# Hybrid encoder layer on one core: both x chunks turned by VectorE blocks and transfers, attention's rows in freed input blocks, queued work weighed by its age

## The chip, the cores and the metric

One NeuronCore of a Trainium2 chip runs the whole layer: a matrix engine (TensorE, PE in the profile), VectorE (DVE), ScalarE (ACT), GpSimd (POOL), and SyncE (SP), whose main job here is to issue transfers. The metric is device microseconds of one execution; the kernel before has a median of 1148.32 us over three runs (1145.85 to 1148.58). One profiled execution of it is read below.

## The reference, cut to what matters

Sequence 256, model width 2048, everything in float32. One layer:

```python
hn = rms_norm(h, g_mix_pre)
q, k, v, xr, yg = split(hn @ w_in, 5 parts of 1024)
attn = neighborhood_attention(q, k, v, rpb)          # 8 heads of 128
rec  = rglru_bidirectional(xr, ...) * gelu(yg)       # conv, gates, forward and backward scan
mixed = concat([rms_norm(attn), rms_norm(rec)]) @ w_out
h = h + rms_norm(mixed)
ff = (silu(fn @ w_ffn_gate) * (fn @ w_ffn_up)) @ w_ffn_down    # fn = rms_norm(h), d_ff 5632
h = h + rms_norm(ff)
h = h + rms_norm(sigmoid(rms_norm(h) @ w_ple_gate) * (p @ w_ple_proj))
```

## The kernel before, in words

**Products.** A float32 product is made of three products of rounded values: the left side and each weight tile are split into a high part (rounded) and a low part (the rest), and hi*hi, lo*hi and hi*lo are added in PSUM. A weight tile is 256 rows by 512 columns (512 KB). It is loaded by SP into one of four raw buffers `wr`; ACT rounds it into `wh` (line 661), DVE subtracts to make `wl` (line 677), and PE uses both in 12 products of 128x512 (lines 715 to 717). There are four pairs of `wh` and `wl`. So a load waits until DVE has split the tile four places ahead of it, and ACT's rounding waits until PE is done with the tile four places ahead. Weight tiles are counted from 0 here, in the order of their use. "Lead" is the time by which a tile's `wl` is ready before PE's first product with it.

**The mixing stage.** The input projection has ten chunks of 512 columns in the order x0 v0 q0 k0 x1 q1 k1 v1 g0 g1; x0 and v0 take turns in tiles 0 to 15, and each later chunk takes eight tiles, up to tile 79. The left side of all of them is `hT_hi`, `hT_lo` (16 blocks of 128 rows). After its last product a chunk is scaled out of PSUM by ACT into `ev` (line 1055, one buffer), and most chunks have to be turned (rows to columns) before they can be used. There are two ways:

- PE turns 128x128 pieces against the identity (line 334, tile `tr`), four pieces for two blocks, into PSUM. x0, x1, k1, g0 and g1 go this way.
- `moved` (lines 340 to 355): DVE turns 32x32 blocks in place (line 343), and 16 small transfers of 32 KB put the blocks in their places in `sq` (line 353, one buffer), all issued by SP. q0, k0 and q1 go this way (`BY_BLOCKS`, line 1028).

A turned x chunk is copied to `xp`, convolved on DVE (`xc`, lines 1106 and 1111), split (`xch`, `xcl`), and its gates are PE products (tile `pg`); their weights are loaded by SP (`av`, line 1083) and split into `gh`, `gl`. Sigmoids, decay, two scans and the sum `hs` follow on ACT and DVE. q and k give scores (`sc`), softmax (`pr`), turned weights of attention (`tr<-ident,pr`), and `po`. When both halves are there, attention's rows are normalised (`attn_norm`) and split: blocks 0 and 1 into `at0`, blocks 2 to 7 into a new pair `attn_hi`, `attn_lo`, which takes the place of `hT_hi`, `hT_lo` as a whole. So its writing waits until the last input product has read them. These rows and the recurrent ones (`rec_hi`, `rec_lo`) are the left side of the output projection, from tile 80 on.

**What sets the order.** Everything is written out once, ahead of time, by a planner (`Plan`, line 91). Streams of work are Python generators that offer their next step with a cost; the planner keeps a clock for PE, DVE, ACT and the transfers, and whenever PE's clock has passed on, it writes every step whose start lies before it, the one with the least start plus `late` first (`_best`, line 152). What it writes is a fixed order for each engine. Small PE work such as `tr`, `pg`, `sc` and `po` is written between weight products once its inputs are planned to be ready. A product costs `MM` = 0.216 us on that clock until the FFN, from where it is 0.2265. A transfer is booked at 150/340 = 0.44 us, and as landed 2.0 us after the last one.

**Pools.** SBUF is nearly full in the mixing stage: its pool `p1` holds `ev` and `sq` once each.

## Time and profile before

| what | value |
|---|---|
| median of three runs | 1148.32 us (1145.85 to 1148.58) |
| span of the profiled execution | 1144.3 us |
| PE busy | 1134.3 us, 99% |
| DVE busy | 945.8 us, 83% |
| ACT busy | 732.1 us, 64% |
| transfers | 269.01 MB, mean 235 GB/s |
| input projection, in the span | to about 255 us |
| output projection | to about 340 us |
| embedding products and the turn to the FFN | 340 to 360 us |
| FFN | to about 1045 us |

The span runs from the first to the last instruction; the median of the runs is 4.0 us above it. PE's instructions overlap in the records (one product starts about every 0.227 us but is shown for 0.39 us), so that PE's busy share hides small pauses; they are found in the waits and in the distances from start to start.

### The profile page before, as it was taken

To read this page: it belongs to the slowest core of one execution; us is meant where nothing else is said; L and a number is where in the kernel's file an instruction comes from. 1 tells how busy PE (TensorE), PEld (TensorE's weight loads), DVE (VectorE), ACT (ScalarE), POOL (GpSimd) and SP (SyncE) were. 2 spreads that over 40 slices of the span, in tenths; PEclk is the share of its full clock that TensorE was granted. 3 is DMA by queue.
4 is the path that set the end of the run, shared out by engine and by line. 5 is a ranking of instruction groups with operands and counts; after the bars stand their busy time and mean duration, and the time that the engine had idled before them with its cause. 6 is when DMAs were issued, how large, how long until landed. Compare 5 with 4: busy or idle time off the path is not lost.

```text
span 1144.3 us, 15197 instructions
## 1 busy us (share of the span) xinstructions
PE 1134.3 (99%) x5175; PEld 942.3 (82%) x5175; DVE 945.8 (83%) x1201; ACT 732.1 (64%) x967; POOL 149.3 (13%) x236
## 2 busy tenths in 40 slices
PE   9999999999999999999999999999999999999997
PEld 7888888888888888888888888888888888888886
DVE  6578697888468779899997898999988888888885
ACT  6777877876447655666566556556564565576674
POOL 0000000000000032132010133232111313100200
PEclk9999999999999999999999999999999999999999
DMA  9867666546685996887877777797797777967862
GB/s 321 288 194 218 180 193 198 167 158 204 208 313 172 300 299 214 230 249 213 279 271 219 260 223 215 249 266 243 258 314 244 229 244 227 285 242 254 257 208 95
DMA packets 110846, 269.01 MB, mean 235 GB/s; under 512 B 36336, under 2 KB 43248, under 8 KB 109360
## 3 DMA queue, kind: packets, MB, share of 16 engines
q1 hardware_dynamic: 96304, 243.17, 63.3%
q0 software_dynamic: 14032, 24.52, 11.2%
q8 instruction: 40, 0.66, 0.2%
q10 hardware_dynamic: 432, 0.35, 0.1%
q14 instruction: 38, 0.31, 0.1%
HBM read 250.17 MB, written 9.44 MB: 227 GB/s over the span
## 4 chain that ended last, share of the span: by engine, by line
PE 92%; DVE 3%; DMA 2%; ACT 2%; issue 1%; SPq 0%; DVEq 0%; ACTq 0%
PE acc L717 23%; PE acc L716 23%; PE acc L715 23%; PE acc L728 7%; PE acc L726 7%; PE acc L727 7%; DVE wl L677 1%; PE tr L334 1%; DMA mg<-part 1%; ACT wh L661 1%; DMA sq<-ev 0%; PE half L2012 0%; PE acc L2012 0%; PE pg L366 0%; PE pg L365 0%
## 5 line engine op out<-in xcount | busy, mean ns | idle before, releaser
L677 DVE TENSOR_TENSOR wl<-wr,wh 128x1024 fp32r<-128x1024 f32 (+1 forms) x300 | 358.9, 1210 | 91.6 <-ACT wh L661 90.2
L661 ACT CAST wh<-wr 128x1024 fp32r<-128x1024 f32 (+1 forms) x300 | 310.8, 1043 | 164.3 <-PE acc L716 112.1
L353 POOL DMA_DIRECT2D mT<-mid x164 | 96.1, 597 | 610.6 <-DMA lower<-in_w_ffn_up 401.1
L716 PE MATMUL acc<-wh,hT_mix_lo 128*128 128x512 f32 x420 | 163.6, 390 | 0.3 <-DVE hT_mix_lo L323 0.3
L715 PE MATMUL acc<-wh,hT_mix_hi 128*128 128x512 f32 x420 | 163.7, 390 | 0.0
L717 PE MATMUL acc<-wl,hT_mix_hi 128*128 128x512 f32 x420 | 163.4, 389 | 0.0
L717 PE MATMUL acc<-wl,hT_hi 128*128 128x512 f32 x320 | 124.5, 390 | 0.0
L715 PE MATMUL acc<-wh,hT_hi 128*128 128x512 f32 x316 | 124.4, 394 | 0.0
L716 PE MATMUL acc<-wh,hT_lo 128*128 128x512 f32 x316 | 123.1, 390 | 0.0
L661 ACT CAST wh<-ple 128x1024 fp32r<-128x1024 f32 (+1 forms) x68 | 68.2, 1008 | 77.4 <-DVE ple L607 47.7
L716 PEld LDWEIGHTS acc<-wh,hT_mix_lo 128*128 128x128 f32 x420 | 78.8, 188 | 17.1 <-DVE hT_mix_lo L323 1.0
L715 PEld LDWEIGHTS acc<-wh,hT_mix_hi 128*128 128x128 f32 x420 | 78.9, 188 | 16.3
L717 PEld LDWEIGHTS acc<-wl,hT_mix_hi 128*128 128x128 f32 x420 | 78.8, 188 | 16.4
L677 DVE TENSOR_TENSOR wl<-ple,wh 128x1024 fp32r<-128x1024 f32 (+1 forms) x68 | 79.2, 1165 | 10.1 <-ACT wh L661 9.7
L717 PEld LDWEIGHTS acc<-wl,hT_hi 128*128 128x128 f32 x320 | 60.0, 188 | 12.8
L716 PEld LDWEIGHTS acc<-wh,hT_lo 128*128 128x128 f32 x316 | 59.4, 188 | 11.6
L715 PEld LDWEIGHTS acc<-wh,hT_hi 128*128 128x128 f32 x316 | 59.4, 188 | 11.4
L630 POOL DMA_DIRECT2D ple<-in_w_ffn_up x27 | 24.1, 892 | 162.9 <-DVE wl L677 121.9
L661 ACT CAST wh<-third 128x1024 fp32r<-128x1024 f32 x33 | 34.7, 1052 | 13.9 <-PE acc L716 8.2
L677 DVE TENSOR_TENSOR wl<-third,wh 128x1024 fp32r<-128x1024 f32 x33 | 40.2, 1219 | 0.7 <-ACT wh L661 0.5
L661 ACT CAST wh<-lower 128x1024 fp32r<-128x1024 f32 x30 | 31.4, 1051 | 13.9 <-PE acc L716 12.4
L677 DVE TENSOR_TENSOR wl<-lower,wh 128x1024 fp32r<-128x1024 f32 x30 | 36.3, 1217 | 1.8 <-ACT wh L661 1.8
(463 smaller groups left out, 2481.1 us busy)
## 6 DMA issues: line engine op xcount, KB each, us to landing
wr<-in_w_in SPq DMA_DIRECT2D x77, 512.0 KB, 4.3
wr<-in_w_ffn_gate SPq DMA_DIRECT2D x73, 512.0 KB, 5.2
wr<-in_w_ffn_down SPq DMA_DIRECT2D x55, 512.0 KB, 5.6
wr<-in_w_ffn_up SPq DMA_DIRECT2D x51, 512.0 KB, 4.8
wr<-in_w_out SPq DMA_DIRECT2D x32, 512.0 KB, 4.4
wr<-in_w_ple_gate SPq DMA_DIRECT2D x30, 512.0 KB, 4.7
lower<-in_w_ffn_up SPq DMA_DIRECT2D x21, 512.0 KB, 5.9
lower<-in_w_ffn_down SPq DMA_DIRECT2D x17, 512.0 KB, 5.7
```

The source lines that it names most:

```text
L334: nc.tensor.transpose(tr[:, b, t * P : (t + 1) * P], e[:, t, sl], ident)
L353: (nc.gpsimd if i in pool else nc.sync).dma_start(dst[32 * j : 32 * j + 32, :, :, i, :], src[32 * i : 32 * i + 32, :, :, j, :],)
L630: nc.gpsimd.dma_start(dst, src, accum_op=ALU.add)
L661: nc.scalar.copy(his[i][:, 0 : src.shape[1], :] if n == 2 else his[i][:, j, :], src)
L677: nc.vector.tensor_tensor(out=los[i][:, m, :], in0=src, in1=f32(his[i][:, m, :]), op=ALU.subtract)
L715: nc.tensor.matmul(accs[t], hi[:, sl], his[i][:, j, :], start=st, stop=False, **group)
L716: nc.tensor.matmul(accs[t], lo[:, sl], his[i][:, j, :], start=False, stop=False, **group)
L717: nc.tensor.matmul(accs[t], hi[:, sl], los[i][:, j, :], start=False, stop=sp, **group)
L726: nc.tensor.matmul(dst, x[0], wh, start=start, stop=False, skip_group_check=seeded)
L727: nc.tensor.matmul(dst, x[1], wh, start=False, stop=False, skip_group_check=seeded)
L728: nc.tensor.matmul(dst, x[0], wl, start=False, stop=stop, skip_group_check=seeded)
```

## The change: what it does

- x0 and x1 are added to `BY_BLOCKS`, so they too are turned by DVE blocks and transfers.
- `ev` and `sq` get a second buffer each (in the pool and in the planner's slots). The room for it comes from the space in SBUF that is reserved for GpSimd's transfer descriptors, which is set to 8192 bytes a partition.
- For all five chunks that are turned by blocks, half of the 16 transfers (`pool=(0, 2)`) are issued by GpSimd instead of SP.
- Attention's rows 2 to 7 are written into blocks 2 to 7 of `hT_hi`, `hT_lo` themselves. Each pair of blocks has an event `ev_used`, set when the last chunk's product with this pair has been written; no new pair is taken.
- The planner lowers `late` of a step by 0.2 times the time that it has been waiting (`age`), until the ninth segment of the output projection. `MM` and `MM4` become 0.2263 and 0.9.

```diff
@@ Plan.__init__
-        self.now = 0.0
+        self.now, self.age = 0.0, 0.2
@@ Plan._best
             late = task.late() if callable(task.late) else task.late
+            late -= self.age * max(0.0, s - task.ready)
             if best is None or s + late < best[0] - 0.05:
@@ layer
-    plan = Plan(wr=R_BUFS, w=W_BUFS, sm=SM_BUFS, acc=4, ev=1, mid=2, bt=2, m2=1, mt=1, sq=1, ...
+    plan = Plan(wr=R_BUFS, w=W_BUFS, sm=SM_BUFS, acc=4, ev=2, mid=2, bt=2, m2=1, mt=1, sq=2, ...
...
-    MM = 0.216
-    MM4 = 0.86
+    MM = 0.2263
+    MM4 = 0.9
@@ products
             if j:
+                if lhs is hT and i >= i_last:
+                    ev_used[kx].t = plan.clk["pe"]
                 free_w(i)
@@ sq_tile
-        return t1["pool"].tile([P, NT, HB, P], F32, tag="sq", name="sq")
+        return t1["pool"].tile([P, NT, HB, P], F32, tag="sq", name="sq", bufs=2)
 
-    BY_BLOCKS = {("q", 0), ("k", 0), ("q", 1)}
+    BY_BLOCKS = {("x", 0), ("x", 1), ("q", 0), ("k", 0), ("q", 1)}
@@ turned
-        eT = yield from moved(e, here, "sq", sq_tile)
+        eT = yield from moved(e, here, "sq", sq_tile, pool=(0, 2))
@@ evac
-                e = t1["pool"].tile([P, NT, N], F32, tag="ev", name="ev")
+                e = t1["pool"].tile([P, NT, N], F32, tag="ev", name="ev", bufs=2)
...
-    ev_in = Event()
+    ev_used = {b: Event() for b in range(0, KD, 2)}
@@ attend
         yield from attn_norm((0,), ra, *at0)
-        yield ev_in
-        at_hi, at_lo = hT_pair("attn")
-        mixT.blocks(at_hi, at_lo, 2, H - 2, 2)
+        mixT.blocks(hT_hi, hT_lo, 2, H - 2, 2)
         for bs in ((2, 6), (4,)):
-            plan.add(attn_norm(bs, ra, at_hi, at_lo), plan.now)
+            plan.add(attn_norm(bs, ra, hT_hi, hT_lo), plan.now)
@@ attn_norm
+            if b:
+                yield ev_used[b]
             yield from split(at_hi[:, sl, :], at_lo[:, sl, :], attnT[:, sl, :], 2 * S)
...
     n_in = len(segs)
+    i_last = len(tiles) - len(KS)
@@ main loop
-            if n == n_in - 1:
-                ev_in.t = plan.clk["pe"]
+            if n == n_in + 8:
+                plan.age = 0.0
@@ kernel
-    nc = bacc.Bacc("TRN2", target_bir_lowering=False, num_devices=1)
+    nc = bacc.Bacc("TRN2", target_bir_lowering=False, num_devices=1, dynamic_dma_scratch_size=8192)
```

The change moves instructions well beyond the lines of the diff, since the planner sets the order. (The diff adds lines, so that line 353 of before is line 354 after, 677 is 678, and so on.)

SP's queue around the turning of x0, before: `wr` are the weight loads, `av` the recurrent gates' weights, `bt` the bias of attention, `sq<-ev` the small transfers, here those of q0.

```order
L578 DMA wr<-in_w_in 128x1024 x11
L1083 DMA av<-in_w_rg_a 128x2x128
L1083 DMA av<-in_w_rg_i 128x2x128
L1083 DMA av<-in_w_rg_a 128x2x128
L1083 DMA av<-in_w_rg_i 128x2x128
L578 DMA wr<-in_w_in 128x1024 x6
L1296 DMA bt<-in_bias 128x2x256 x2
```

The same place after the change, from the same weight load on:

```order
L579 DMA wr<-in_w_in 128x1024 x8
L354 DMA sq<-ev 32x8x32 x2
L579 DMA wr<-in_w_in 128x1024
L354 DMA sq<-ev 32x8x32
L579 DMA wr<-in_w_in 128x1024
```

Five more rounds of one transfer and one or two loads follow, and only then the four `av` loads. So SP's half of x0's transfers (eight) stands one by one between weight loads 20 to 27, and the gates' weights are asked for behind load 28 instead of load 23. GpSimd's half has a queue of its own, which stood empty there.

DVE in a stretch of the second half of the input projection, before, from the split of tile 63 on (`ig`, `hs`, `th` belong to the recurrent part of x1, `kl` and `pr` to attention):

```order
L677 TENSOR_TENSOR wl<-wr,wh 128x1024
L1175 TENSOR_TENSOR ig<-ig,r 128x512 x2
L317 TENSOR_TENSOR kl<-tr,kh 128x512
L1179 SCALAR_TENSOR_TENSOR hs<-av,ig 128x256
L1183 SCALAR_TENSOR_TENSOR th<-av,ig 128x256
L1179 SCALAR_TENSOR_TENSOR hs<-av,ig 128x256
L1183 SCALAR_TENSOR_TENSOR th<-av,ig 128x256
L1315 SCALAR_TENSOR_TENSOR pr_500<-sc,bt 128x512
```

After the change these scans stand behind the splits of tiles 69 and 70, and attention's rows follow within four tiles more:

```order
L678 TENSOR_TENSOR wl<-wr,wh 128x1024
L1186 SCALAR_TENSOR_TENSOR th<-av,ig 128x256
L1182 SCALAR_TENSOR_TENSOR hs<-av,ig 128x256
L1209 TENSOR_TENSOR ssa<-ssa,sqa 128x256
L1186 SCALAR_TENSOR_TENSOR th<-av,ig 128x256
L678 TENSOR_TENSOR wl<-wr,wh 128x1024
L1211 TENSOR_TENSOR ssa<-ssa,sqa 128x256
L1153 TENSOR_TENSOR hs<-hs,th 128x512
L1109 TENSOR_SCALAR xc<-xp,vec 128x256
L1114 SCALAR_TENSOR_TENSOR xc<-xp,vec,xc 128x256
```

So the recurrent work of the first half of x1 has moved six to seven tiles back, into the stretch of tiles 68 to 77, and the rows `hT_lo<-attnT,hT_hi`, which had stood behind tile 82 as `attn_lo<-attnT,attn_hi`, now stand behind tiles 75 to 77.

More of the change, by code (lines that the diff above doesn't have):

```diff
@@ L249, in layer @@
     ps = ctx.enter_context(tc.tile_pool(name="ps", bufs=4, space=bass.MemoryType.PSUM))
-    plan = Plan(wr=R_BUFS, w=W_BUFS, sm=SM_BUFS, acc=4, ev=1, mid=2, bt=2, m2=1, mt=1, sq=1, x=0, T0=1, T1=1, T4=1, **{f"{s}{j}": n for s, m, n in (("p", 5, 1), ("t", 4, 0)) for j in range(m)}, wr0=1, w0=1)
+    plan = Plan(wr=R_BUFS, w=W_BUFS, sm=SM_BUFS, acc=4, ev=2, mid=2, bt=2, m2=1, mt=1, sq=2, x=0, T0=1, T1=1, T4=1, **{f"{s}{j}": n for s, m, n in (("p", 5, 1), ("t", 4, 0)) for j in range(m)}, wr0=1, w0=1)
     def f32(t):
```

## The prediction, made before the changed kernel ran

> **What bounds the kernel now.** I read the page first, for the engines and the chain that ended last.
>
> ```profile
> span 1144.3 us, 15197 instructions
> PE 1134.3 (99%) x5175; PEld 942.3 (82%) x5175; DVE 945.8 (83%) x1201; ACT 732.1 (64%) x967; POOL 149.3 (13%) x236
> PE 92%; DVE 3%; DMA 2%; ACT 2%; issue 1%; SPq 0%; DVEq 0%; ACTq 0%
> ```
>
> PE is busy for 99% of the span and carries 92% of the chain. A busy PE can hide pauses, so I read its waits over the whole span next.
>
> ```profile
> PE final L2098 <- ACT diag L2096: 2.3, 1, 2.3
> PE warm L2193 <- POOL ones L299: 1.1, 1, 1.1
> PE acc L703 <- ACT wh L661: 0.8, 1, 0.8
> PE acc L716 <- DVE hT_mix_lo L323: 0.3, 1, 0.3
> PE tr L334 <- DVE h L1598: 0.2, 1, 0.2
> PE acc L716 <- DVE hT_ffn_lo L323: 0.2, 1, 0.2
> ```
>
> The first three are the end and the start, which the change leaves alone. None of the waits lies in the input projection, where most of the change lies. So what can be won there is PE's own work and little else; what can be lost depends on how close the other engines come to making PE wait. That is read from the busy times by stage (columns: stretch, length, then busy us and instructions of PE, PE's weight loads, DVE, ACT and POOL, the granted clock, the transfers' share and GB/s).
>
> ```profile
> 44.00:148.00 104.00, 104.00 (x504) 87.50 (x503) 78.72 (x125) 81.13 (x119) 0.00 (x0) 1.00 0.68 202
> 190.00:215.00 25.00, 24.93 (x135) 21.24 (x134) 24.31 (x42) 19.06 (x33) 0.00 (x0) 1.00 0.59 186
> 362.00:970.00 608.00, 608.00 (x2684) 503.46 (x2683) 533.50 (x607) 363.22 (x409) 132.00 (x200) 1.00 0.81 249
> ```
>
> PE is full at full clock. In 44 to 148 us DVE is busy for 78.7 of 104, but in 190 to 215 us for 24.31 of 25; the third row is the FFN, for later. The lead of the weights shows how close this comes (timeline: start, length):
>
> ```profile
> 98.20 1.22 DVE L677 TENSOR_TENSOR wl<-wr,wh 128x1024 fp32r<-128x1024 f32 x1
> 99.13 0.39 PE L715 MATMUL acc<-wh,hT_hi 128*128 128x512 f32 x1
> 99.81 0.39 PE L715 MATMUL acc<-wh,hT_hi 128*128 128x512 f32 x1
> 205.07 1.23 DVE L677 TENSOR_TENSOR wl<-wr,wh 128x1024 fp32r<-128x1024 f32 x1 [0.34 <-ACT wh L661]
> 206.87 0.39 PE L715 MATMUL acc<-wh,hT_hi 128*128 128x512 f32 x1
> ```
>
> Three products start in 99.81 - 99.13 = 0.68 us, so a tile's twelve take 2.72 us. Tile 33 is split at 99.42 and used at 99.81, a lead of 0.39 us; tile 66 has 206.87 - 206.30 = 0.57 us. The stage is bound by PE, with DVE and ACT twice within half a microsecond of stopping it.
>
> **The change, part by part.** *PE's turning of x0 and x1 goes.* PE turns `ev` 24 times instead of 40; the sixteen of x0 and x1 are gone.
>
> ```profile
> L334 PE MATMUL tr<-ident,ev x40: 270/272/273, 49.7 to 260.1; 128*128 128x128 f32 x40
> 49.74 0.60 PE L334 MATMUL tr<-ident,ev 128*128 128x128 f32 x4
> 49.90 0.44 PE tr L334 x4
> ```
>
> The 272 ns overlap; on the chain a run of four costs 0.44 us. Sixteen are 1.76 us, all on PE: **-1.76**. The other products stay the same in number and size, some at other places.
>
> *What replaces it.* For each x chunk one block transpose on DVE and sixteen small transfers; ACT's copies to `xp` stay, from SBUF now.
>
> ```profile
> L343 DVE STREAM_TRANSPOSE ev<-ev x3: 1235/1236/1245, 76.3 to 161.7; 128x1024 f32<-128x1024 f32 x3
> L353 SPq DMA_DIRECT2D sq<-ev x48: 585/608/805, 77.5 to 178.2; - x48
> L353 POOL DMA_DIRECT2D mT<-mid x164: 582/582/1001, 402.9 to 1066.7; - x164
> sq<-ev SPq DMA_DIRECT2D x48, 32.0 KB, 3.6
> mT<-mid POOLq DMA_DIRECT2D x164, 32.0 KB, 5.4
> av<-in_w_rg_i SPq DMA_DIRECT2D x8, 128.0 KB, 4.5
> L661 ACT CAST wh<-wr 128x1024 fp32r<-128x1024 f32 x75 | 77.5, 1050 | 23.9 <-PE acc L716 17.9 <-DMA wr<-in_w_in 2.3 <-DVE wl L677 1.5
> ```
>
> DVE gets 2 x 1.24 = 2.5 us more in a stage whose first half leaves a quarter of it free: nothing by itself. SP issues 40 of the small transfers instead of 48, at 0.61 us, so its queue is shorter. GpSimd, idle in this stage, issues 40 at 0.58 us. The price is in *when* the blocks are there. For x0: SP's eighth transfer stands behind load 26, which waits for the split of tile 22, which waits for PE to finish tile 18. Tile 16 can start at 49.74 without the turning, so tile 18 ends three tiles later, at 57.9; tile 22 is rounded and split by 57.9 + 1.05 + 1.22 = 60.2, and the transfer, issued at 60.6, lands 3.6 us later at 64.2. GpSimd's eight wait for no weight tile; behind the transpose, which stands right after tile 16's split, they take 8 x 0.58 + 5.4 = 10.0 us: SP's half decides. The copies and the convolution (eight operations of about 0.5 us) end at about 69. The gates' weights come later: behind load 28, which tile 24's split frees two tiles later than load 26, at about 65.6, four issues of half a microsecond, 4.5 us to land: 72.4, rounding 1.05 and splitting 1.22: 74.7. PE wants them at tile 25: 49.74 + 9 x 2.72 = 74.2. That is **0.5 us** of new wait; gates' weights that land half a microsecond sooner make it nothing, and 5.4 us in place of 4.5 makes it 1.4. The planner booked such things tightly, as its `MARGIN` is 0.4 us; I take **+0.4**.
>
> *Second buffers of `ev` and `sq`* cost nothing; they let a chunk be scaled while the one before is in flight. The ring of GpSimd's descriptors is halved; no row shows a wait for room in it, and the largest burst here is eight transfers: 0.
>
> *DVE's full stretch moves and grows.* Behind tiles 68 to 77 there now stand, by the order: 11 operations of 128x1024, 22 of 128x512 or scans, one reciprocal and some 20 others of 128x256.
>
> ```profile
> L677 DVE TENSOR_TENSOR wl<-wr,wh 128x1024 fp32r<-128x1024 f32 x74 | 88.9, 1219 | 18.3 <-ACT wh L661 18.3
> L317 DVE TENSOR_TENSOR pl<-tr,ph 128x512 fp32r<-128x512 f32 x8 | 5.5, 688 | 2.1 <-ACT ph L315 2.1
> L1111 DVE SCALAR_TENSOR_TENSOR xc<-xp,vec,xc 128x256 f32<-128x256 f32 x24 | 11.5, 480 | 0.2
> L1198 DVE RECIPROCAL rb_attn<-rb_attn x1: 1746/1746/1746, 241.5 to 241.5; 128x256 f32<-128x256 f32 x1
> L1168 DVE SCALAR_TENSOR_TENSOR r<-r,th 128x512 f32<-128x512 f32 x8 | 5.2, 689 | 7.5 <-ACT r L1166 7.5
> ```
>
> That is 13.4 + 15.1 + 1.7 + 20 at 0.48 or less, 9 = 39 us (the scans at the price of 128x512), against PE's 10 x 2.72 + 4.4 = 31.6 (two gate products of twelve at half a product's 0.227, eight pieces turned for 0.9, a sum for some 0.6). DVE falls back by 7 to 8 us there. The lead before it is at most 3 x 2.72 - 1.05 - 1.22 = 5.9 us, since a tile's rounding waits for PE to end the fourth tile ahead, and up to 3.7 more for small PE work in those three tiles (a `po`, a `tr`, a `pg`): 6 to 9.6. So it comes out near nothing, as tiles 63 to 69 of before do (lead 0.57). The waits inside it decide: `r` waited 7.5 us on ACT in four places, 1.9 in each. From 0 to 3; most of these waits were absorbed before, so **+0.5**.
>
> *Attention's rows in freed blocks.* Before, they were written only after the last input product; now from tile 75 on. PE never waited for them (no such row above), so this wins nothing; it fills DVE's stretch, which is counted.
>
> *Age, and a truer clock for PE.* Their effect is the order. One thing goes with it: a pause of PE in softmax's turning, behind a weight split on DVE.
>
> ```profile
> 209.27 0.31 PEld L334 LDWEIGHTS tr<-ident,pr 128*128 128x128 f32 x3 [0.30 <-DVE pr L1333]
> ```
>
> Attention's `tr` now come in pairs behind finished rows: **-0.3**, or 0. The other place is the turn to the FFN (the chain's pieces of DVE first, then PE's starts):
>
> ```profile
> 350.77 1.13 DVE wl L677
> 352.29 0.41 DVE hT_mix_lo L323
> 350.37 0.48 PE L715 MATMUL acc<-wh,hT_mix_hi 128*128 128x512 f32 x1
> 350.82 0.50 PE L716 MATMUL acc<-wh,hT_mix_lo 128*128 128x512 f32 x1
> 352.09 0.39 PE L715 MATMUL acc<-wh,hT_mix_hi 128*128 128x512 f32 x1
> 352.74 0.50 PE L716 MATMUL acc<-wh,hT_mix_lo 128*128 128x512 f32 x1 [0.27 <-DVE hT_mix_lo L323]
> ```
>
> Starts lie 0.23 us apart where nothing is waited for; here the first and second pair of rows lie 0.45 and 0.65 apart, and the product behind each another 0.1 late: 0.9 us of pauses, the second because a `wl` stands ahead of the second `hT_mix_lo`. After, this `wl` stands ahead of the first `h` instead: the second pause goes (0.5), while the first `hT_mix_lo` and the third group of `tr` come about 0.3 later each. I take 0, between -0.9 and +0.9.
>
> Sum: -1.76 + 0.4 + 0.5 - 0.3 + 0 = -1.2 us, a span of 1143.1 and, with the 4.0 us between span and median, **1147.1 us**. From the bounds: -1.76 - 0.3 - 0.9 = -3.0 to -1.76 + 1.4 + 3 + 0.9 = +3.5, thus 1145.3 to 1151.8.
>
> **A rule that speaks against it.** All 164 transfers that GpSimd issued in the FFN took 582 ns at the median and 1001 at most, beside a DVE that was busy for 533.5 of 608 us. The Trainium skill, "SBUF — State Buffer", section "Who interferes with whom", says that a DVE instruction with one SBUF source can take the port that GpSimd shares, and GpSimd is then shut out to its end. By it, GpSimd's issues could each wait for one of the convolution's or softmax's one-source operations here, none of which is longer than the 0.48 us of the `xc` row, so eight come up to 3.8 us later; x0, where SP's half decides, would stay as it is, and the other chunks would move that much towards rival B. The FFN has hardly any such operations on SBUF, so no row here shows it.
>
> **The rivals.** *A: no new wait at all.* The planner now knows PE's real pace, so the order could be simply better: all pauses that I named go and none comes: -3.0, 1145.3. For it: the old order, planned with a PE 5% too fast, made one pause of 0.3 us in 250. Against it: two leads under 0.6 us shown above, so a new order of the same work at a higher load hardly stays free. The three runs of before spread over 2.7 us, so about half of this case would be measured as over 0.3% faster.
>
> *B: blocks land too late and hold up ACT* — slower. GpSimd's half is booked at 8 x 0.44 + 2.0 = 5.5 us; the rows say 8 x 0.58 + 5.4 = 10.0, 4.5 more. The cast or copy of a block that hasn't landed stands ahead of the next weights' rounding on ACT.
>
> ```profile
> ACT qh L315 <- DMA sq<-ev: 2.5, 1, 2.5
> ```
>
> This wait of 2.5 us, for q0 at about 96 us, was borne, down to the lead of 0.39 shown above. One of 4.5 there stops PE for 4.5 - 2.5 - 0.4 = 1.6 us. Over five chunks that is 8 us: 1148.3 - 2.1 + 8 = 1154. It decides from four chunks on (6.4 - 2.1 = 4.3 us, over 0.3%). Against it: GpSimd's 5.4 us come from the FFN, where the transfers are 0.81 busy (0.59 to 0.68 here), and x0 showed SP's half as the later one. *C: the turning was hidden anyway* can't be: PE has no idle time to hide it in.
>
> **How the numbers follow.** A difference of 0.3%, 3.4 us, is about what a measurement of this kernel tells from none. The forecast (1147.1, own range 1145.3 to 1150) has a chance of 0.52, A 0.30, B 0.18. Faster: half of A, 0.15, and 0.02 of the forecast's edge: 0.17. Slower: nine tenths of B, 0.16. The rest, 0.67, is within 0.3%. The range goes from A less half the runs' spread, 1143.9, to 1151.8, short of B's centre.
>
> **What would show it.** Right: `tr<-ident,ev` x24 and no turning by PE ahead of tile 57; PE's busy time down by 1.8 us; waits of PE between 44 and 275 us under 1.5 us in all, the first at the gates of x0 near 74 us, others at tiles 73 to 78 (about 225 to 245 us). B would show as ACT's waits on `sq<-ev` of 4 us and more, with PE waiting for `wl` behind them. Wrong at the root would be a PE whose products start at another distance than 0.227 us, or a change in the FFN after 420 us, where the order is the same.

## The result, and the profile after

The changed kernel takes **1153.51 us** at the median of six runs (1149.42 to 1159.74), the kernel before 1147.51 us in the six runs beside it (1145.85 to 1148.74). The ratio is 1.0064, with a 95% interval of 1.0047 to 1.0080: slower by 0.6%, where no measurable difference had been forecast. The profiled execution took 1152.8 us, with this head of the page:

```profile
span 1151.0 us, 15278 instructions
PE 1135.9 (99%) x5159; PEld 942.7 (82%) x5159; DVE 947.8 (82%) x1203; ACT 730.8 (63%) x967; POOL 172.3 (15%) x276
```

The span is 6.7 us longer than before. PE's busy time has not fallen by the 1.8 us of the sixteen turnings that are gone; it has risen by 1.6, which already says that something stretched PE's own instructions. The waits of PE over the span (who, at which line, for whom: us in total, times, longest):

```profile
PE acc L718 <- DVE wl L678: 2.8, 2, 2.2
PE pg L366 <- DVE xcl L318: 1.7, 1, 1.7
PE tr L335 <- ACT ev L1058: 1.4, 2, 1.2
```

None of the three is in the list of before. They lie at three places, which I follow one by one. A pause is told below as the distance from start to start, less what it is where nothing is waited for: 0.23 us for a weight product, 0.12 for a gate product and 0.11 for a turning, which are smaller.

**First place, near 113 us.** k0's blocks were turned on DVE at 99.05 to 100.29. The timeline of the changed kernel, first SP's queue, then ACT, DVE and PE (start, length; in brackets the idle time before it and what ended it):

```profile
100.32 0.60 SPq L354 DMA_DIRECT2D sq<-ev  x1
101.80 5.81 SPq L354 DMA_DIRECT2D sq<-ev  x7
104.81 1.05 ACT L662 CAST wh<-wr 128x1024 fp32r<-128x1024 f32 x1 [1.36 <-DMA wr<-in_w_in]
111.71 0.62 ACT L316 CAST kh<-sq 128x512 fp32r<-128x512 f32 x1 [5.85 <-DMA av<-in_w_rg_a]
112.24 1.04 ACT L662 CAST wh<-wr 128x1024 fp32r<-128x1024 f32 x1
112.36 0.69 DVE L318 TENSOR_TENSOR kl<-sq,kh 128x512 fp32r<-128x512 f32 x1 [2.34 <-DMA av<-in_w_rg_i]
113.89 1.22 DVE L678 TENSOR_TENSOR wl<-wr,wh 128x1024 fp32r<-128x1024 f32 x1
112.53 0.39 PE L717 MATMUL acc<-wh,hT_lo 128*128 128x512 f32 x1
115.16 0.80 PE L718 MATMUL acc<-wl,hT_hi 128*128 128x512 f32 x1 [2.24 <-DVE wl L678]
```

ACT reaches the cast of k0 at 105.86 and stands there for 5.85 us. (The row names `av`, but the cast reads only `sq`: in the trace the last of k0's sixteen transfers landed at 111.54, and the first `av` at 111.74, when the cast had begun.) PE then stops for the split of tile 38, for 2.63 - 0.23 = 2.40 us. That tile's rounding doesn't stand behind the cast: it is the one at 104.81, ahead of it. What stands behind is the split, in DVE's queue: `kl`, k0's low part, needs the cast, and DVE idles 2.34 us for it; two `xc` operations and then the split follow. The rounding behind the cast, at 112.24, is tile 39's; that tile is split by 117.78 and needed at 122.48, in time. Then the granted clock drops. In the windows below, each row is a stretch: start and end, length, busy us and instructions of PE, PE's loads, DVE, ACT and POOL, the granted clock, the transfers' share, GB/s.

```profile
111.78:115.19 3.41, 1.17 (x7) 0.63 (x5) 2.79 (x5) 2.96 (x4) 0.00 (x0) 1.00 0.95 291
115.19:118.60 3.41, 3.41 (x8) 2.76 (x9) 3.41 (x5) 2.57 (x3) 0.00 (x0) 0.50 0.56 197
193.69:197.11 3.42, 1.73 (x14) 1.42 (x13) 3.42 (x5) 2.91 (x7) 0.00 (x0) 1.00 0.64 193
```

For 3.41 us behind the pause PE works at half clock: eight products there where fifteen would fit, some 1.7 us more. PE's "busy" time holds that loss, so it doesn't show as a wait. This place costs 4.1 us.

**Second and third place, near 179 and 194 us** (ACT, then PE; ACT, DVE, then PE):

```profile
177.26 0.62 ACT L316 CAST qh<-sq 128x512 fp32r<-128x512 f32 x1 [2.44 <-DMA wr<-in_w_in]
179.99 0.33 PE L335 MATMUL tr<-ident,ev 128*128 128x128 f32 x1 [1.19 <-ACT ev L1058]
190.45 1.05 ACT L316 CAST gh<-av 128x1024 fp32r<-128x1024 f32 x1 [5.10 <-DMA av<-in_w_rg_i]
195.74 0.39 PE L366 MATMUL pg<-xcl,gh 128*128 128x256 f32 x1 [1.69 <-DVE xcl L318]
```

The chain of waits between 160 and 195 us names the way: q1's and x1's transfers, asked for together from 160.5 on, hold SP's queue and land up to 6.7 us after their issue; q1's cast holds up ACT (its row names a weight load, but the cast reads only `sq`); k1's scaling (`ev`), which PE wants to turn, comes late (pauses of 1.35 and 0.47 us); and x1's gates' weights, asked for last, land at 190.4 (a pause of 1.85 us). Together the three places cost 4.1 + 1.8 + 1.85 = 7.8 us. With the sixteen turnings saved (-1.76), 1.05 us of pauses in tiles 73 to 76, and some 0.7 us of pauses gone (softmax's, and a part of those at the turn to the FFN), that makes 6.4 of the 6.7 us.

Why are the blocks late? The rows of transfers that group the issues while k0's are under way, in the changed kernel (KB each, median us from issue to landing; 98 to 109 us):

```profile
sq<-ev SPq DMA_DIRECT2D x8, 32.0 KB, 6.2
sq<-ev POOLq DMA_DIRECT2D x8, 32.0 KB, 6.6
```

In the kernel before the same chunk, with all sixteen in SP's queue (105 to 123 us), had this row:

```profile
sq<-ev SPq DMA_DIRECT2D x16, 32.0 KB, 2.8
```

There they were spread from 106.0 to 122.4 us, between weight loads. The windows of the twelve us behind the turning of k0, the kernel before and then the changed one, columns as above:

```profile
106.00:118.00 12.00, 12.00 (x64) 10.26 (x63) 7.62 (x8) 9.99 (x17) 0.00 (x0) 1.00 0.82 233
```

```profile
100.00:112.00 12.00, 12.00 (x54) 9.84 (x54) 9.92 (x16) 4.78 (x7) 4.60 (x8) 1.00 0.96 196
```

The transfer engines are 0.96 busy instead of 0.82 while they move less. GpSimd's half saves SP's issuing time, but part of that gain comes back as landing time: from the turning's end to the cast, k0's blocks take 111.7 - 100.3 = 11.4 us; the planner had booked 5.5. The landings in the trace show what they stand behind. The weight load that SP asked for at 101.42, among them, has this row:

```profile
wr<-in_w_in SPq DMA_DIRECT2D x1, 512.0 KB, 7.0
```

It landed at 108.47. The three small transfers issued before it landed by 105.6; the thirteen issued after it, by either queue, landed between 108.9 and 111.5, nearly all in the order of their issue and 0.2 us apart.

### The profile page after: what moved, and what is told of

Read it like the earlier page. It is cut to its first block, busy times and chain, and to the rows that moved or that the text cites. A ratio compares the mean times of both kernels' runs of the same rounds, so it can differ in the third digit from the quotient of the medians.

```text
span 1151.0 us, 15278 instructions
## 1 busy us (share of the span) xinstructions
PE 1135.9 (99%) x5159; PEld 942.7 (82%) x5159; DVE 947.8 (82%) x1203; ACT 730.8 (63%) x967; POOL 172.3 (15%) x276
## 4 chain that ended last, share of the span: by engine, by line
PE 90%; DVE 3%; DMA 3%; ACT 3%; issue 1%; SPq 1%; DVEq 0%; ACTq 0%; POOL 0%; POOLq 0%
PE acc L718 22%; PE acc L716 22%; PE acc L717 22%; PE acc L731 7%; PE acc L730 7%; PE acc L729 7%; DMA sq<-ev 2%; DVE wl L678 1%; ACT wh L662 1%; PE tr L335 1%; DMA av<-in_w_rg_i 1%; DMA wr<-in_w_in 0%; PE warm L2197 0%; PE half L2016 0%; PE acc L2016 0%
## 5 line engine op out<-in xcount | busy, mean ns | idle before, releaser
L718 PE MATMUL acc<-wl,hT_hi 128*128 128x512 f32 x368 | 144.2, 393 | 2.8 <-DVE wl L678 2.8
L716 PE MATMUL acc<-wh,hT_hi 128*128 128x512 f32 x364 | 143.5, 394 | 0.0
L717 PE MATMUL acc<-wh,hT_lo 128*128 128x512 f32 x364 | 142.3, 391 | 0.0
L718 PEld LDWEIGHTS acc<-wl,hT_hi 128*128 128x128 f32 x368 | 69.5, 189 | 18.7 <-DVE wl L678 4.0
L717 PEld LDWEIGHTS acc<-wh,hT_lo 128*128 128x128 f32 x364 | 68.8, 189 | 13.9
L716 PEld LDWEIGHTS acc<-wh,hT_hi 128*128 128x128 f32 x364 | 68.9, 189 | 13.4
L354 POOL DMA_DIRECT2D sq<-ev x40 | 23.2, 589 | 146.2 <-DVE ev L344 98.1
L662 ACT CAST wh<-third 128x1024 fp32r<-128x1024 f32 x33 | 34.7, 1053 | 13.7 <-PE acc L717 8.0
```

Source lines behind the costliest of these rows:

```text
L354: (nc.gpsimd if i in pool else nc.sync).dma_start(dst[32 * j : 32 * j + 32, :, :, i, :], src[32 * i : 32 * i + 32, :, :, j, :],)
L662: nc.scalar.copy(his[i][:, 0 : src.shape[1], :] if n == 2 else his[i][:, j, :], src)
L716: nc.tensor.matmul(accs[t], hi[:, sl], his[i][:, j, :], start=st, stop=False, **group)
L717: nc.tensor.matmul(accs[t], lo[:, sl], his[i][:, j, :], start=False, stop=False, **group)
L718: nc.tensor.matmul(accs[t], hi[:, sl], los[i][:, j, :], start=False, stop=sp, **group)
```

## The experiments

**Theory T**: blocks come later than the order has booked; the cast or copy of a block stands in ACT's queue ahead of the next weights, and SP's queue passes the rest on to the gates' weights. (At the first place the weights are held up in DVE's queue instead, behind `kl`, as said; the runs below test that late blocks are the cause, and only their traces show by which queue.) **Rival O**: the new order itself, made with the age term and a slower PE clock, overfills ACT and DVE, whatever the transfers do. Later a **rival P** came in: the small transfers slow the weight loads down. All ratios are to the kernel before, in runs on the same chip.

| run | what | median us | ratio (95% interval) |
|---|---|---|---|
| 1 | changed kernel, no small transfers | 1145.80 | 0.9989 (0.9980 to 0.9998) |
| 2 | SP issues all | 1166.81 | 1.0172 (1.0157 to 1.0187) |
| 3 | GpSimd issues all | 1166.07 | 1.0175 (1.0158 to 1.0192) |
| 4 | before, with pauses put in | 1208.09 | a single run |
| 5 | truer booking of blocks | 1148.27 | 1.0013 (1.0004 to 1.0022) |
| 6 | x by PE again | 1147.45 | 1.0006 (0.9997 to 1.0015) |
| 7 | no age | 1160.72 | 1.0126 (1.0112 to 1.0140) |
| 8 | SP issues all and is booked so | 1168.08 | 1.0186 (1.0172 to 1.0202) |
| 9 | x without transfers | 1148.92 | 1.0023 (1.0014 to 1.0031) |
| 10 | q and k without transfers | 1146.19 | 0.9994 (0.9985 to 1.0004) |
| 11 | truer booking, x1 by PE | 1150.65 | 1.0032 (1.0022 to 1.0043) |
| 12 | truer booking, both x by PE | 1146.32 | 0.9992 (0.9984 to 1.0001) |
| 13 | old PE clock in the planner | 1150.37 | 1.0033 (1.0020 to 1.0045) |
| 14 | before, with x by blocks alone | 1171.03 | 1.0206 (1.0191 to 1.0221) |
| 15 | truer booking of gates too | 1151.99 | 1.0042 (1.0028 to 1.0056) |

### Runs 1, 9 and 10: the transfers taken out, the order kept

```diff
@@ moved (run 1; in runs 9 and 10 for x alone, for q and k alone)
+                if take == "sq":
+                    mT = e
+                    continue
                 if mT is None:
                     mT = tile_of()
...
+        if take == "sq":
+            return e.rearrange("p t (k q) -> p k t q", q=P)
```

> The changed kernel with its order on PE, DVE, ACT and of all weight loads kept, but the five chunks turned by blocks are read from ev itself, without the eighty small transfers (so blocks stand in wrong places: the placing is left out). Theory T (transfers that land 5 to 7 us after their issue, booked at 2.0, hold up ACT and, through SP's queue, the gates' weights and weight tiles): the pauses of PE near 113, 178 and 194 us go, and with the first one the stretch at half clock behind it; 1.9 + 2.4 + 1.8 + 1.9 = 8 us of 1153.5, so 1145 to 1147. Rival O (the new order itself, made with a slower PE clock and the age term, overfills DVE and ACT whatever the transfers do): pauses stay at the same places, 1151 to 1154.

The same order on PE, DVE and ACT, without the eighty transfers, takes 1145.8 us. (These three runs leave out the placing of blocks, so what they compute is not the layer.) All three places are gone. Its only wait of PE above 0.3 us in the mixing stage:

```profile
PE acc L723 <- DVE wl L683: 0.6, 1, 0.6
```

That is the pause in DVE's full stretch at tiles 73 to 76 (line 683 is line 678 of the changed kernel). So O falls for these 7.8 us: the same order holds once the blocks are there. This run is also what the change could have won if turning by blocks were free: 0.1%, about 1.3 us.

> The changed kernel, its order on PE, DVE and ACT kept, but only x0 and x1 are read from ev itself, without their 32 transfers (their blocks stand in wrong places); q0, k0 and q1 keep theirs. If the lateness adds up over chunks that follow one another (q0 takes the lead of the weights, k0 finds none left; q1 and x1 in one burst): the pause near 113 us and the slow clock behind it stay (2.4 + 1.9 us), those at 178 to 194 us shrink below 1 us, 1149 to 1151. If the two new chunks alone cost the time: all pauses go as in the run without any transfer, 1146.

> The counterpart: the order of the changed kernel, x0 and x1 by transfers, but q0, k0 and q1 read from ev itself (their blocks stand in wrong places). If the lateness of q0 and k0 makes the first pause and that of q1 the second: no pause near 113, one of under 1 us near 178, 1146 to 1148. If x1's own blocks hold up ACT: the pauses at 178 to 194 us stay, 3 to 4 us, 1149 to 1151.

With x0's and x1's transfers out but q0's, k0's and q1's left, the first place stays and the others go:

```profile
PE acc L723 <- DVE wl L683: 3.0, 3, 1.7
ACT kh L316 <- DMA av<-in_w_rg_i: 5.6, 1, 5.6
```

The time is 1148.92. The clock didn't drop this time (pauses of 0.83 and 1.88 us, in two pieces). The other way round, with x by transfers and q and k in place, nothing of it is left, and the time is 1146.19. So it is not x's own blocks that PE waits for. At the first place it is k0's, with q0's late before them; no run takes out q0's or k0's alone. At the others it is q1's, which became late because x1's were asked for at the same time (either of the two taken out, the pauses there go).

### Runs 2, 3 and 8: who issues

```diff
@@ moved (run 2: SP all; run 3: GpSimd all, the order of all else kept)
-                (nc.gpsimd if i in pool else nc.sync).dma_start(
+                (nc.gpsimd if i in pool and take != "sq" else nc.sync).dma_start(    # run 2
+                (nc.gpsimd if i in pool or take == "sq" else nc.sync).dma_start(     # run 3
@@ turned (run 8: SP all, and the planner knows it)
-        eT = yield from moved(e, here, "sq", sq_tile, pool=(0, 2))
+        eT = yield from moved(e, here, "sq", sq_tile)
```

> The changed kernel, same order on PE, DVE and ACT, but SP issues all sixteen transfers of a chunk, GpSimd none. If SP's queue is what passes the lateness on to weight loads and gates' weights (theory T in its SP form): eight issues more of 0.6 us per chunk ahead of them, 4.9 us later each, so three pauses grow by 2 to 5 us each, 1158 or more. If GpSimd's half is the one that lands late (rival B as it was predicted): the pauses shrink, 1148 to 1150. Rival O: within 1 us of 1153.5.

> The changed kernel, same order on PE, DVE and ACT, but GpSimd issues all sixteen transfers of a chunk, so SP's queue holds only loads. Theory T in its SP form: the loads behind leave up to 4.9 us sooner per chunk, the pauses near 113 and 194 us (gates' weights) go, 1147 to 1150. If the landing of the blocks themselves decides (sixteen issues of 0.58 and a landing, 9.3 + 5 = 14 us after the turning): ACT waits longer for the blocks, 1156 or more. Rival O: within 1 us of 1153.5.

Both are 13 us slower than the changed kernel, so halves are better than either queue alone, and neither queue is "the" late one. In run 2 k0's blocks land 2.0 us after their issue, but the last one is issued so late that the cast waits 8.3 us; in run 3 it waits 10.5:

```profile
sq<-ev SPq DMA_DIRECT2D x16, 32.0 KB, 2.0
ACT kh L316 <- DMA sq<-ev: 8.3, 1, 8.3
PE acc L718 <- DVE wl L678: 8.1, 6, 4.4
PE tr L335 <- ACT ev L1058: 5.9, 1, 5.9
```

```profile
119.27 0.62 ACT L316 CAST kh<-sq 128x512 fp32r<-128x512 f32 x1 [10.50 <-DMA sq<-ev]
PE acc L718 <- DVE wl L678: 9.0, 5, 6.8
```

The large pauses stand at the first two of the three places, with smaller ones of up to 1.8 us ahead of them, and grow with the lateness of the blocks. That is theory T's dose and effect: waits of k0's cast of 0, 5.85, 8.3 and 10.5 us (run 1, the changed kernel, runs 2 and 3) go with PE pauses near 115 us of 0, 2.4, 4.6 and 7.0. In runs 2 and 3, too, the tile that PE stops for, 38, was rounded ahead of that cast, and its split stands behind `kl` on DVE. My two forms of T for these runs ("SP's queue" against "the blocks' own landing") were put too sharply: it is the arrival of the sixteenth block, by whichever queue. That the 1166 of run 3 fits "1156 or more" and that of run 2 "1158 or more" says no more than that.

> The changed kernel with all sixteen transfers of a chunk issued by SP and booked so (9.1 us for a chunk instead of 5.5), so that the order knows of the longer queue. Casts come three to seven tiles later than in the changed kernel. If what is wrong is the booking of halves at 5.5 us: still 13 us late against 9.1 booked, 4 us instead of 5, pauses of 2 to 6 us, 1148 to 1153. If SP's queue itself is the limit (32 issues one behind the other for q1 and x1, 20 us): as slow as the run in which SP issued all without the planner knowing, 1160 or more.

The pauses moved instead of shrinking. With the longer queue booked, x1's recurrent part comes so late that the output projection has to wait for it (`pb_rec` sums the squares for the norm of the recurrent rows):

```profile
PE pb_rec L1196 <- DVE ssr L1211: 10.5, 1, 10.5
PE acc L716 <- ACT rec_hi L316: 4.3, 1, 4.3
```

SP's queue is too long for five chunks, as the second half of the expectation had it; the place is not the one that I had in mind.

### Runs 5 and 15: the order made with truer transfer times

```diff
@@ moved (runs 5 and 15)
-                yield ("pool" if i in pool else "dma", COST["move"], None, first, None)
+                yield ("pool" if i in pool else "dma", 0.6 if take == "sq" else COST["move"], None, first, None)
...
+        if take == "sq":
+            plan.now += 3.0
         done(here)
@@ load_gates (run 15 only)
         yield dma(512)
+        plan.now += 2.5
```

> The changed kernel with one thing altered in the planner: a small transfer of a turned chunk is booked at 0.6 us instead of 0.44 and the last one as landed 5.0 us after it instead of 2.0, near what the traces show. The casts of k0 move from behind the rounding of tiles 39 and 40 to 42 and 43, those of q1 from 58 and 59 to 63 and 64. Theory T (blocks are in time or not by what was booked; ACT's queue passes the lateness on to the weights): the pauses near 113, 178 and 194 us go, 1145 to 1148. Rival O (DVE and ACT are overfilled by the new order): the work is only moved, pauses of about the same sum at other places, 1151 to 1155. Rival P (the transfers themselves slow the weight loads down): pauses with ACT waiting for weight tiles stay, 1150 or more.

(The tiles in it are counted from one.) The three places are gone, as T has it, and no cast waits for a block. What is left of PE's waits in the mixing stage is smaller, 3 us in five places (one, near 189 us, still stands behind x1's gates' weights); two of the rows:

```profile
PE acc L720 <- DVE wl L680: 1.3, 2, 0.7
PE acc L719 <- DVE rec_lo L318: 1.0, 1, 1.0
```

The loss against the kernel before falls from 0.64% to 0.13%, 1153.5 to 1148.3 us: most of it was booking. The upper end of T's range was missed by 0.3 us, and rival O is right in so far as later casts make something else late. ACT's waits for weight tiles stay at 15.0 us in all (15.2 in the changed kernel, and 5.3 without transfers), but none of PE's five waits stands behind one of them, which leaves little to rival P.

> The changed kernel with the truer booking of the blocks (0.6 us each, landed 5.0 after) and the gates' weights booked as landed 4.5 us after their issue instead of 2.0. If the pauses left by the truer booking of blocks alone (4.9 us between 188 and 290 us, 1148.3) are gates' weights that land late: they fall to 2 or less, 1145 to 1147. If they come from the recurrent rows being late for the output projection, because five chunks by transfers take longer however they are booked: 1147.5 to 1150.

The second alternative in kind, 2 us above its range. PE runs from 40 to 287 us without a pause over 0.25 us, and then meets recurrent rows that aren't there:

```profile
PE acc L718 <- ACT rec_hi L316: 4.6, 1, 4.6
```

Behind it the clock is at half for 6.8 us, and the time is 1152.0. So the booking is not the whole of it. When five chunks are moved, x1's chain (turning, transfers, convolution, gates, two scans, norm) either pushes into ACT's queue too early or ends too late for the output projection.

### Runs 6, 7, 13 and 14: the parts

```diff
@@ run 6                                   @@ run 7
-    BY_BLOCKS = {("x", 0), ("x", 1), ...  -        self.now, self.age = 0.0, 0.2
+    BY_BLOCKS = {("q", 0), ("k", 0), ...  +        self.now, self.age = 0.0, 0.0
@@ run 13 (and MM4 0.9 to 0.86)            @@ run 14, on the kernel before
-    MM = 0.2263                           -    BY_BLOCKS = {("q", 0), ("k", 0), ("q", 1)}
+    MM = 0.216                            +    BY_BLOCKS = {("x", 0), ("x", 1), ("q", 0), ...
```

> The changed kernel without its first part: x0 and x1 are turned by PE again; q0, k0 and q1 keep blocks, GpSimd's half, the buffers, the age and PE's clock. PE's own work grows by 1.76 us. If the extra chunks are the cause (two bursts more, q1's and x1's one behind the other): pauses under 2 us in all, 1147 to 1149. If the booking of a chunk at 5.5 us is the cause whichever chunk it is: the pause at k0 near 113 us stays, 2 to 4 us, that behind q1 goes, 1150 to 1153.

1147.45: without its first part, the change costs nothing that can be measured. k0's blocks are late here too, but the weights had a larger lead, and PE waits 0.3 us for the score itself, and 1.4 us for softmax's rows behind it:

```profile
ACT kh L316 <- DMA sq<-ev: 5.2, 1, 5.2
PE tr L335 <- DVE pr L1336: 1.4, 2, 1.2
```

The pause "of 2 to 4 us at k0" that the second alternative gave didn't come. A late chunk costs only what the lead at that point doesn't cover. Here tile 38, the last one split before k0's cast, was ready 6.3 us ahead of the first product that reads its `wl`. In the changed kernel tiles 36 and 37, split just before that cast, were ready 0.17 and 0.34 us ahead; in run 1, the same order without transfers, 1.70 and 1.85. So the new order itself leaves little lead there, and late transfers took the rest. That q0's late cast (a wait of 3.4 us on ACT near 86 us) is part of it is likely, as k0's turning starts 1.8 us later than in run 1, but was not run by itself.

> The changed kernel without the age term, everything else kept. The casts of k0 stand behind the rounding of tile 40 instead of 39 and 40, the others up to four tiles earlier. Theory T: transfers are booked as before, so blocks are late at other or the same places, 1150 to 1156. Rival O in its form that the age term makes the order bad: 1145 to 1148.

1160.72, above both ranges given. The age term is no cause of the loss; without it the same parts are worse by 7 us, with 5.4 us behind one late scaling of a chunk:

```profile
PE acc L716 <- ACT ev L1058: 5.4, 1, 5.4
```

> The changed kernel with the planner's old PE clock (MM 0.216, MM4 0.86), everything else kept. Theory T: with PE booked 5% too fast each later tile is planned earlier than it can be, which leaves blocks more real time before their casts, but the casts themselves stand one to three tiles earlier (q1 and x1 behind the 57th to 60th rounding): pauses of a similar sum, 1150 to 1156. If the truer PE clock is what made the order too tight: 1145 to 1148.

1150.37, at the lower end of T's range. With the old clock the pauses are others again (the largest, 2.65 us at 258 us, stands behind ACT's `av` and `r`, with no transfer in it). An order made with the truer clock isn't the better one here; with one order of each this says nothing general.

> The kernel before with one thing changed: x0 and x1 are added to the chunks turned by blocks; one buffer each, SP issues everything, no age, old PE clock. PE works 1.76 us less. Theory T: SP's queue gets 32 issues of 0.6 us more, and x1's and q1's chunks come one behind the other with one buffer: blocks later than booked by 4 us in five places instead of three, and x1's recurrent rows late, 1152 to 1165. If blocks for x cost nothing by themselves: 1145 to 1147.

1171.03, above the range given: x by blocks alone, added to the kernel before, costs 24.5 us. The copy of x1's blocks holds ACT for 8.36 us, the next chunk can't be scaled out of PSUM, and PE waits 11.3 us for an accumulator; later it waits 8.1 us for attention's rows, and around these two waits the granted clock is at half for 13.7 and 10.2 us:

```profile
183.04 0.62 ACT L1073 COPY xp<-sq 128x512 f32<-128x512 f32 x1 [8.36 <-DMA sq<-ev]
PE acc L715 <- ACT ev L1055: 11.3, 1, 11.3
PE acc L715 <- ACT at_hi L315: 8.1, 1, 8.1
```

So the first part is what costs, and the others (second buffers, GpSimd's half, rows written in place, age, PE's clock) together take 17.5 of its 24.5 us back, where the prediction had most of them at nothing.

### Runs 11 and 12: candidates

```diff
@@ truer booking as in run 5, and
-    BY_BLOCKS = {("x", 0), ("x", 1), ("q", 0), ("k", 0), ("q", 1)}
+    BY_BLOCKS = {("x", 0), ("q", 0), ("k", 0), ("q", 1)}    # run 11
+    BY_BLOCKS = {("q", 0), ("k", 0), ("q", 1)}              # run 12
```

> A candidate: the changed kernel with the truer booking (0.6 us for a transfer, landed 5.0 after the last), and x1 turned by PE again, x0 by blocks. Against the truer booking with both: PE works 0.88 us more, but the recurrent rows of x1 come earlier, so that its pauses of 4.9 us between 188 and 290 us should fall to 2 or less: 1145.5 to 1147.5, by theory T. If every new order of this work brings some 4 us of pauses: 1148 to 1150.

> The other candidate: both x chunks turned by PE, everything else of the change kept, with the truer booking. PE's own work is that of the kernel before. The run with the old booking had pauses of 2.8 us behind late blocks and rows of k0 between 117 and 143 us; with the truer booking these should go: 1145 to 1147 by theory T. If the booking matters only where five chunks are moved: 1147 to 1148 as with the old one.

Run 11 is slower, at 1150.65, outside both of its ranges, with 2.6 us of pauses at x1's gates (1.6 us on their rounding, 0.8 on the low part). Run 12, 1146.32, has no pause of PE over 0.2 us between 40 and 300 us, as T said, and a span of 1143.8. But its interval reaches 1.0001, so it isn't shown to be faster than the kernel before. (One of its eleven executions took 4092.59 us. It is left out of the ratio, and nothing in the record explains it.) No version here beats the kernel before by more than a measurement can tell; run 1 shows that there was little more than 0.1% to win.

### Run 4: what a pause costs beside itself

```diff
@@ lo_stream, on the kernel before
+    PAUSE = {86: 5, 100: 6, 150: 4, 175: 5, 200: 6, 225: 7, 250: 8, 275: 5, 300: 6, 325: 7}
-                nc.vector.tensor_tensor(
-                    out=los[i][:, m, :], in0=src, in1=f32(his[i][:, m, :]), op=ALU.subtract
-                )
+                for _ in range(1 + (PAUSE.get(i, 0) if j.stop == 2 else 0)):
+                    nc.vector.tensor_tensor(
+                        out=los[i][:, m, :], in0=src, in1=f32(his[i][:, m, :]), op=ALU.subtract
+                    )
```

> The kernel before with ten pauses of PE put in: the low part of a weight tile is worked out four to eight times over again on DVE (1.22 us each) at two tiles of the output projection and eight of the FFN. It measures what a pause costs beside its own length. If the drop of the granted clock seen after the changed kernel's pause of 2.4 us (0.5 for 3.4 us, 1.9 us more) is what a pause of that length brings: pauses over about 2 us are each followed by a stretch at 0.5 of 3.4 us, those under it by none. If it was by chance: only pauses over 3.4 us or none show it. Time 15 to 35 us over the kernel before.

The run took some 61 us more than the kernel before, where 15 to 35 had been expected. The pauses came out between 1.1 and 6.2 us. The three under 2 us (1.1, 1.3, 1.6) have no slow stretch behind them; each of the eight over 3 us has one, of 3.41 us or of 6.83; none lay between, so this run alone doesn't test pauses of 2 to 3 us. The granted clock changes only at moments that are whole multiples of 3.413 us apart, in this run (stretches of 225.28, 47.79 and 6.83 us are 66, 14 and 2 such steps) as in the others. Stretches of one such step, the first from run 2 and the others from run 4, columns as above:

```profile
185.20:188.61 3.41, 1.56 (x7) 0.94 (x5) 1.22 (x1) 1.05 (x1) 0.00 (x0) 1.00 0.80 214
669.13:672.55 3.42, 1.32 (x6) 0.75 (x4) 3.32 (x4) 1.05 (x1) 0.00 (x0) 1.00 0.23 95
672.55:675.96 3.41, 0.00 (x0) 0.00 (x0) 3.34 (x3) 0.00 (x0) 0.00 (x0) 0.50 0.00 0
508.70:512.12 3.42, 0.41 (x2) 0.37 (x3) 3.35 (x4) 0.00 (x0) 3.42 (x7) 1.00 0.33 58
512.12:515.53 3.41, 3.41 (x10) 2.67 (x9) 3.41 (x4) 1.04 (x1) 1.13 (x2) 0.50 0.41 66
```

In the first PE idles for 1.85 of 3.41 us, and the next step (188.61 to 192.02) still has full clock; with 2.10 idle (669.13) and with 3.0 (508.70) the next is at half. The changed kernel adds 2.24 idle, then half, and 1.69 idle, then full. In the seventeen traces, between 20 and 1130 us, no step at full clock goes against this: with up to 1.85 us idle the next one is at full clock, with 2.10 or more at half. Run 13's pause of 2.65 us near 259 us speaks most for the step, and not the pause, being what counts, as it lies across two steps (1.62 and 0.87 us idle) and no slow stretch follows:

```profile
256.99:260.40 3.41, 1.79 (x8) 1.13 (x7) 1.67 (x3) 3.39 (x5) 0.00 (x0) 1.00 0.45 144
260.40:263.81 3.41, 2.54 (x11) 2.11 (x12) 1.81 (x2) 3.38 (x5) 0.00 (x0) 1.00 0.44 144
```

So a pause of some 2 us costs itself or 1.7 us more, by where it falls among the steps. That would also spread a kernel's runs, and the changed kernel's six lie 10 us apart where those of before lie 3; that this is why, was not shown.

## Why the prediction was wrong, point by point

The forecast was 1147.1, range 1143.9 to 1151.8; measured 1153.5, outside of it. It came out as rival B had it (1154, given 0.18), and by late blocks, as B said. The 4.0 us that the forecast added between span and median were too much: on record an execution takes 1.8 us more than its own span (1152.8 against 1151.0), and the rest was a profiled execution of before that was shorter than the median.

- **PE's turning, -1.76: right.** The changed kernel's group of `tr<-ident,ev` counts 24, PE has exactly sixteen products fewer (5159 for 5175), and without transfers (run 1) the whole gain is 1.3 us (0.2 to 2.3), against the -1.2 of the sum. So the sum fits a change whose transfers cost nothing.
- **"What replaces it", +0.4 at x0's gates: the step that failed.** No pause came at x0's gates, near 74 us: their weights had landed at 70.8 and not at 72.4. x0 was worked out with care, and it is the chunk that did no harm. The step took one chunk for all five, and took 3.6 us for the landing from a kernel in which SP issued alone. With GpSimd issuing at the same time it was 6.2 to 6.6 for k0, 11.4 us from turning to cast in place of the 5.5 booked. In the sum, cover was counted at no other chunk than x0, so the late casts of q0, k0 and q1 stood in it at nothing. Run 10, in which these three need no transfers, is 7.3 us faster than the changed kernel; that is what was missing.
- **Rival B: right in the cause, wrong in the way on and in the argument against it.** B had the next weights' rounding on ACT stand behind the cast. At the first place that rounding (tile 39) was in time, and PE waited for a split on DVE behind `kl`; only at the second place did ACT's queue pass a block's lateness on, to k1's scaling. The argument against B was that transfers were 0.59 to 0.68 busy in this stage. That was read as a mean over long stretches of the old order; behind k0's turning the engines were 0.82 busy in that order already, and 0.96 in the new one. Its price, 1.6 us for each of five chunks from four chunks on, was the right sum by the wrong parts, and so by luck: two clusters of late blocks (q0 and k0, q1 and x1) cost 2.4 and 3.7 us of pauses, and 1.7 us of slow clock came on top, which nothing in the prediction had. The lead in that price was misread too: 0.39 us is the distance to tile 33's first product, which reads only `wh`; the first that reads `wl` starts at 100.27, which leaves 0.85. Nor was GpSimd's half alone the late one (runs 2 and 3).
- **DVE's full stretch, +0.5 (0 to 3): right in place, 1.05 us in size.** With or without transfers, PE waits for the split of tiles 73 and 74: the first product that reads their `wl` starts 0.05 us behind it.
- **Softmax's pause, -0.3, and the turn to the FFN, 0:** the first is gone, as said; the second gained 0.4, within its bounds.
- **Second buffers, GpSimd's half, rows in place, age at nothing:** wrong in the other direction. Without them, and with PE's old clock, x by blocks costs 17.5 us more than the changed kernel (run 14). Of the single parts only GpSimd's half (13 us, run 2), the age (7 us, run 7) and PE's clock (3 us the other way, run 13) were taken out by themselves.
- **The rule on the shared port.** GpSimd's forty issues took 582 ns at the median and 773 at most, so the up to 3.8 us a chunk that the prediction worked out from the Trainium skill, "SBUF — State Buffer", section "Who interferes with whom", didn't occur here. But the rule was hardly put to the test: of DVE's operations from one source, TENSOR_SCALARs and turnings overlapped these issues seven times, with 622 ns for the longest issue, and none of the convolution or of softmax ran beside one.

What stays open: how much of the longer landing comes from two queues at once and how much from GpSimd's own way. GpSimd alone had landings of 5.4 us at the median for k0 (run 3), SP alone 2.0 (run 2), both together 6.2 and 6.6. The traces point to the weight loads between: in run 2 thirteen of k0's transfers were issued by SP one behind the other with no load among them, and the transfer engines were 0.59 busy; in run 3 SP, free of blocks, asked for three weight loads and the gates' weights in that time, and each block issued after a weight load landed after it. No run changes this alone.

## What to carry to other kernels

A transfer that feeds an in-order engine costs nothing only while the work behind it has lead to spare, so count the lead at every place where such a transfer is awaited, on the engine that waits and on the next one that needs its result, and take the landing time from a stretch that is as full as the new one will be. Issuing from a second queue shortened the issue here and lengthened the landing; book the arrival of the last piece, and measure it again after the change. Where an order is planned from booked times, changing a block's way from an engine to transfers needs the booking to be right first (1153.5 to 1148.3 us here), and even then the longer chain has to end somewhere.

## What the runs showed of the hardware that was not expected

- **The clock falls after less than a window of idling.** PE idle for 2.10 us within one 3.41 us step was enough for the next step at half clock (run 4); 1.85 us was not (run 2). The Trainium skill, "TensorE: Matmul & The Clock Gate", section "HAM oscillation — how this bites in real kernels", puts it as a rule to have no idle gap over some 3.4 us. Here the traces differ: the bound lies between 1.85 and 2.10 us in a step, and the changed kernel's pause of 2.4 us was enough.
- **Landing times of small transfers depend on what was issued around them.** k0's sixteen transfers of 32 KB landed in 2.0 to 2.8 us from SP alone, in 5.4 from GpSimd alone, and in over 6 from either once GpSimd issued half of them. Over all eighty the medians lie closer: 3.4 (SP alone), 5.2 (GpSimd alone), 5.4 and 4.9 (halves of SP and GpSimd). A small transfer issued right behind a weight load landed right behind it: three of x0's in the changed kernel, issued by SP at 55.6, 58.3 and 60.9 us, each landed 0.2 us after the load that SP had issued just before.
